# The three-branch merge of a hybrid decoder layer: 24 ordinary tiles with operands split once, in place of twelve seven-product pairs

## The chip, the cores and the metric

The kernel runs on one core of a Trainium2 chip. The metric is the device time of one launch in microseconds. Three runs of the kernel before took 1910.48, 1914.8 and 1914.9 us (median 1914.8). The engines are named as the profile names them: PE is TensorE's matmul and PEld its weight load, DVE is VectorE, ACT is ScalarE, POOL is GpSimd, SP is SyncE, which here only issues DMAs.

## The reference, cut to what matters

One decoder layer is computed for 1024 prompt tokens and 32 sample tokens, 1056 columns in all, with 1024 model channels:

```
h = rmsnorm(x);  proj = h @ w_in        # feeds three mixers and the gates
oa = attention(...)                     # 512 channels
ob = gated short convolution(...)       # 512 channels
oc = gated DeltaNet(...)                # 512 channels
gates = sigmoid(gl)                     # 3 x 1024 channels
merged = gates[0]*(oa @ w_br_a) + gates[1]*(ob @ w_br_b) + gates[2]*(oc @ w_br_c)
x = x + merged @ w_o
x = x + conv_mlp(rmsnorm(x));  y = rmsnorm(x)
```

The line `merged = ...` is the stage that the change touches. Each branch product takes 512 input channels to 1024 output channels. All data is float32.

## The kernel before, in words

Data stands with channels on the 128 partitions and the 1056 columns in a row. A matmul takes a 128x128 piece of weights and streams columns past it. To keep float32 accuracy every operand x is split in two fp32r numbers: hi, a rounded copy written by ACT (`split`, L217), and lo = x - hi, written by DVE or POOL (L218). One product is then three matmuls: hi by hi, hi by lo, lo by hi.

There are two ways to multiply. The ordinary one is `proj` and `products` (L325): an output tile of 128 channels, three groups of 352 columns, for each group 3 matmuls per 128 input channels into one of three PSUM banks named `mm`, and an evacuation that the caller gives. Its weights come by `job`: `w_load` fetches a tile into one of two buffers `wr`, `w_split` splits it on ACT and POOL into one of two buffers `wh` and one of two `wl`; `run_jobs` loads two tiles ahead and splits one ahead, and `look` does the same from inside another stage.

The other is the class `Pairs` (L1429). It takes two output tiles at a time, cuts weights, operand and output in halves, and forms seven block products in place of eight (`PIECES`). For that it needs sums and differences of weight blocks (`produce`, L1386 to L1392), of operand blocks (`build`, L1315, split in L1305 and L1306), and of the products: three of the seven are first copied to SBUF by ACT (L1438) and added to others by DVE (`summed`, L1457). A product here is 264 columns wide.

Before the merge come nine pairs of gate tiles, the last of them named G26; after it come eight ordinary tiles for `w_o` (`wo_job`), then the MLP, whose up-projection is again pairs. The merge before (`merge_pair`) goes through branch b, then c, then a (numbers 1, 2, 0), four pairs each, twelve in all. A pair has 7 pieces x 2 column halves x 6 matmuls. `load_operand` builds the blocks of a branch beforehand; `load_gate` fetches the gates from DRAM. For each output quarter DVE multiplies the product with the gate (L2007); for c and a POOL adds it to the running sum `macc` (L2013); in branch a ACT and DVE split the sum into `mh` and `ml` (L2020, L2021), the operand of `w_o`. `MADD` and `MLO` say which weight sums and which weight splits of the merge are DVE's; the others are POOL's.

The order on each engine is set by a scheduler that works from the order in which the program emits the instructions, with higher priority for evacuations and weight splits; each engine then works through its list in that order. SP issues all these DMAs from one queue in order. Buffers in SBUF are 46 slots, and a DMA into a slot waits until its last reader is done. Small side work (`bg`, the lanes) is woven in by `bg.tick`.

Of the kernel before, what the change touches and what calls it, by code (L numbers as in the profile page):

```python
# [9 lines left out]
ALU = mybir.AluOpType  # L10
# [145 lines left out]
DPAHEAD, DPADD, DPLO, DTICK = 3, (1, 2, 3, 4), (0,), 6  # L156
HGAP, HSTART = (0.0, 1.5), 12
KEPT = 4
MAHEAD, MADD, MLO = 4, (1, 2), (0, 2, 4, 6)
ORDER = """  # L160
d4 hbd q0 d5 d6 dpairs d7 D0 D2 D8 D10 delta
v k q1 q2 q3 attn_in attn g10 g11 g12 g13 g14
# [11 lines left out]
def trunk(tc, A, O, cst_d):  # L174
# [1119 lines left out]
    def pieces(nk):  # L1294
        return {piece: [None] * (nk // 2) for piece in PIECES}

    def build(bs, p, vp, vq, wait, gap=0):

        t, ta = grab([128, T])
        b11, b12, b21, b22 = vp[0][:, :HT], vp[0][:, HT:T], vq[0][:, :HT], vq[0][:, HT:T]  # L1300
        t1, t2 = t[:, :HT], t[:, HT:T]

        def put(piece, src, eng):
            w = grab([128, T], F32R)
            nc.scalar.copy(w[0][:, :HT], src)  # L1305
# [24 lines left out]
        put("t4", t1, nc.vector)  # L1330
        for x in (ta, vp[1], vq[1]):
            x.drop()
# [119 lines left out]
    def summed(ps, x, more):  # L1452

        if x is None:
            return ps
        dst = (mm_ps() if limit[0] < 4 else bg_ps())[:, :HU] if more else ps
        nc.vector.tensor_tensor(dst, ps, x, op=ALU.add)  # L1457
        return dst
# [397 lines left out]
        return whole_pair(lambda which, t: to_dram(g_d[b][m + which], t), AF.Tanh, 0.5)  # L1856

    def last_gates(j):
        if j + gp.ahead == 6:
            merge_start()  # L1860
        if j == 4:
            load_gate(0)

    def last_d(j):
        if j + dpp.ahead >= 6:
# [56 lines left out]

    ops = {}

    def spare():

        return 2 if at["n"] >= mg.first else 5

    def load_operand(b):

        bs = ops[b] = pieces(4)
        if b == order[0][0]:
            vs = [None] * 4
            for t in range(4):
                yield room2(3)
                vs[t] = grab([128, T])
                dma(vs[t][0], br_d[b][t])
            yield bg.arrived()
            both = [build(bs, p, vs[p], vs[p + 2], lambda: room2(4)(), 0.0) for p in range(2)]
            while both:  # L1940
                for g in both:
                    w = next(g, both)
                    if w is both:
                        both = []
                    else:
                        yield w
        else:
            for p in range(2):
                yield lambda: ready[b]() and room2(3 + spare())()
                vs = [grab([128, T]) for _ in range(2)]  # L1950
                for v, t in zip(vs, (p, p + 2)):
                    dma(v[0], br_d[b][t])
                yield bg.arrived()
                yield from build(bs, p, *vs, lambda: room2(2 + spare())(), 4.5)
        bump(f"op{b}")

    ready = {0: lambda: done.get("att", 0) == 2 * NB + 1, 2: lambda: done.get("oc", 0) == 4}

    mh, ml, macc = [None] * 8, [None] * 8, [None] * 8
    gate = {}  # L1960
    order = [(b, m) for b in (1, 2, 0) for m in range(0, 8, 2)]
    wbr = (A["w_br_a"][0], A["w_br_b"][0], A["w_br_c"][0])
    mg = Pairs(4, [wbr[b][:, m * 128:m * 128 + 256].rearrange("(k p) c -> p k c", p=128) for b, m in order], MAHEAD, 4, MADD, MLO, 6)

    def load_gate(i):
        if i < len(order):
            b, m = order[i]
            for x in (m, m + 1):
                bg.until(room2(1))
                gate[b, x] = grab([128, T])  # L1970
                dma(gate[b, x][0], g_d[b][x])

    def merge_start():
        bg.until(room2(2))
        ms = mg.scratch = [grab([128, SLOT]) for _ in range(2)]
        mg.es = [x[0][:, 0:3 * HU].rearrange("p (a b) -> p a b", b=HU) for x in ms]
        mg.s = [x[0][:, 3 * HU:3 * HU + 256].rearrange("p (a b) -> p a b", b=128) for x in ms]
        mg.load(0)
        mg.produce(0)
        mg.produce(1)  # L1980

    def merge_pair(i):
        b, m = order[i]

        def fn():
            if i == 0:
                for j in range(2, MAHEAD):
                    mg.produce(j)
                sb.drop(16)
                mg.load(1)  # L1990
                sf = ff["states"] = grab([128, 836])
                ff["sf"] = sf[0][:, 0:704].rearrange("p (c r) -> p c r", r=16)
                ff["cw"] = sf[0][:, 704:836]
                bg.add(ffn_in())
            if i % 4 == 0 and i < 8:
                bg.add(load_operand(order[i + 4][0]))
            tt, gt = nc.vector.tensor_tensor, nc.gpsimd.tensor_tensor
            if b == 1:
                for x in (m, m + 1):
                    bg.until(room2(1))  # L2000
                    macc[x] = grab([128, T])

            def out(which, c0, ps, x, more):
                ps = summed(ps, x, more)
                cc = slice(c0, c0 + HU)
                g, acc = gate[b, m + which][0], macc[m + which][0]
                nc.vector.scalar_tensor_tensor((acc if b == 1 else g)[:, cc], g[:, cc], 1.0, ps, op0=ALU.add, op1=ALU.mult)  # L2007
                if b == 1:
                    return
                if c0 % HT == 0:  # L2010
                    return
                cc = slice(c0 - HU, c0 + HU)
                gt(acc[:, cc], acc[:, cc], g[:, cc], op=ALU.add)  # L2013
                if b == 0:
                    if c0 > HT:
                        for y in (mh, ml):
                            bg.until(room2(1))
                            y[m + which] = grab([128, T], F32R)
                    h, l = mh[m + which][0], ml[m + which][0]
                    nc.scalar.mul(h[:, cc], acc[:, cc], 0.5)  # L2020
                    nc.vector.scalar_tensor_tensor(l[:, cc], acc[:, cc], 0.5, f32(h[:, cc]), op0=ALU.mult, op1=ALU.subtract)  # L2021

            def before(piece):
                bg.until(lambda: b in ops and ops[b][piece][1] is not None)

            def after(j, piece):
                if j == 3:
                    load_gate(i + 1)
                if i % 4 == 3:
                    for x in ops[b][piece]:  # L2030
                        x[2].drop()
                if i + 1 == len(order) and j + mg.ahead >= 6:
                    look()

            bg.until(lambda: b in ops)
            mg.run(i, ops[b], out, after, before)
            for x in (m, m + 1):
                gate.pop((b, x))[1].drop()
                if b == 0:
                    macc[x][1].drop()  # L2040
            if i + 1 == len(order):
                for x in mg.scratch:
                    x[1].drop()
        return fn

    mg.first = len(jobs)
    for i in range(len(order)):
        jobs.append((None, -1, lambda wh, wl, fn=merge_pair(i): fn()))

    x1, vs = [None] * 8, {}  # L2050
    ff = {}
# [419 lines left out]
```

## Time and profile before

| | |
|---|---|
| profiled execution | 1915.73 us |
| its span, first to last instruction | 1914.0 us |
| PE busy | 1782.4 us (93%) |
| DVE, ACT, POOL busy | 64%, 43%, 58% |
| last gate pair ends, merge begins | about 938 us |
| last of the merge | about 1104 us |
| `w_o` tiles end | 1188.7 us |

The page's 40 slices are 47.9 us each; the merge fills slices 20 to 22 (counted from 0, 957 to 1101 us) and the end of slice 19. A group row of the trace gives line, engine, operation, output and inputs by name, shapes and count, then busy time, mean time of one, and the idle time before it with what ended it. "Idle before" is only of interest on the engine that sets the end.

### The profile page before, as it was taken

How to read it: one execution, taken by the hardware profiler on the slowest of the kernel's cores; microseconds unless marked ns; L12 is line 12 of the kernel's file. 1: busy time of each engine (PE TensorE's matmuls, PEld its weight loads, DVE VectorE, ACT ScalarE, POOL GpSimd, SP SyncE). 2: the span in 40 equal slices, each digit the busy share in tenths (PEclk: the TensorE clock that was granted, in tenths of full speed). 3: DMA queues.
4: the chain of work that ended last, by engine and by line, in shares of the span. 5: the costliest groups of instructions: out<-in, count | busy, mean ns of one | idle time of the engine just before them, and what ended most of it. 6: DMA issues, size and time to landing. Idle time of an engine off the chain costs nothing.

```text
span 1914.0 us, 34344 instructions
## 1 busy us (share of the span) xinstructions
PE 1782.4 (93%) x13006; PEld 1735.1 (91%) x13006; DVE 1234.3 (64%) x2122; ACT 824.1 (43%) x1780; POOL 1113.7 (58%) x1041
## 2 busy tenths in 40 slices
PE   5889989898999997999988899999999999989997
PEld 4789989798999996999987899999999999989997
DVE  5578812364478779421899956778777778764334
ACT  5445522321244434344653445544554454454433
POOL 3245633334333239886668745988887989434542
PEclk9999999896999997999999999999999999999999
DMA  6312597656556533643462343445454343595513
GB/s 222 98 46 79 186 295 214 176 143 145 152 161 169 150 101 123 238 170 114 164 241 84 108 138 132 129 152 179 142 173 148 126 142 133 224 360 195 180 51 108
DMA packets 293302, 300.84 MB, mean 157 GB/s; under 512 B 56516, under 2 KB 224944, under 8 KB 293120
## 3 DMA queue, kind: packets, MB, share of 16 engines
q1 hardware_dynamic: 233648, 261.94, 42.4%
q10 hardware_dynamic: 59488, 36.70, 6.7%
q8 instruction: 102, 1.67, 0.4%
q14 instruction: 64, 0.52, 0.1%
HBM read 205.30 MB, written 95.28 MB: 157 GB/s over the span
## 4 chain that ended last, share of the span: by engine, by line
PE 44%; DVE 8%; issue 3%; POOL 2%; ACT 2%; DMA 2%; SPq 0%; ACTq 0%; DVEq 0%; POOLq 0%
PE mm L1429 17%; PE bgps L1429 13%; PE mm L325 5%; PE bgps L2347 2%; PE bgps L2349 2%; PE bgps L2348 2%; PE mm L2348 1%; PE mm L2347 1%; PE mm L2349 1%; DVE slot L2007 1%; DVE bgps L1457 1%; DVE slot L1315 1%; DVE wh L218 1%; DVE wl L218 1%; DVE slot L1306 1%
## 5 line engine op out<-in xcount | busy, mean ns | idle before, releaser
L325 PE MATMUL mm<-slot,wh 128*128 128x352 f32 x1920 | 487.6, 333 | 22.1 <-ACT slot L1203 11.8
L325 PEld LDWEIGHTS mm<-slot,wh 128*128 128x128 f32 x1920 | 343.2, 193 | 30.0 <-ACT slot L1203 12.7
L325 PE MATMUL mm<-slot,wl 128*128 128x352 f32 x960 | 317.4, 331 | 1.9 <-POOL wl L218 1.9
L1429 PE MATMUL mm<-slot,wh 128*128 128x264 f32 x1536 | 219.6, 294 | 31.0 <-ACT slot L1438 10.8
L1429 PEld LDWEIGHTS mm<-slot,wh 128*128 128x128 f32 x1536 | 204.7, 197 | 37.0 <-ACT slot L1438 12.7
L1429 PE MATMUL mm<-slot,wl 128*128 128x264 f32 x1464 | 200.7, 287 | 7.7 <-DVE wl L218 4.2
L218 POOL TENSOR_TENSOR wl<-slot,wl 128x512 fp32r<-128x512 f32 (+1 forms) x116 | 154.7, 1334 | 83.0 <-ACT wl L217 62.9
L1429 PEld LDWEIGHTS mm<-slot,wl 128*128 128x128 f32 x1464 | 187.6, 190 | 10.4 <-DVE wl L218 5.0
L218 POOL TENSOR_TENSOR wh<-slot,wh 128x512 fp32r<-128x512 f32 (+1 forms) x103 | 134.1, 1302 | 96.1 <-ACT wh L217 83.9
L325 PEld LDWEIGHTS mm<-slot,wl 128*128 128x128 f32 x960 | 185.2, 193 | 4.1 <-POOL wl L218 2.4
L217 ACT CAST slot<-slot 128x528 fp32r<-128x528 f32 (+4 forms) x212 | 130.5, 636 | 127.0 <-DVE slot L1824 27.9
L218 POOL TENSOR_TENSOR wl<-wr,wh 128x1024 fp32r<-128x1024 f32 x38 | 95.4, 2511 | 152.2 <-ACT wh L217 152.1
L218 DVE TENSOR_TENSOR slot<-slot 128x528 fp32r<-128x528 f32 (+3 forms) x117 | 121.4, 1052 | 88.9 <-ACT slot L217 81.1
L218 POOL TENSOR_TENSOR slot<-slot 128x512 fp32r<-128x512 f32 (+3 forms) x95 | 133.4, 1410 | 77.6 <-ACT slot L217 77.5
L1429 PE MATMUL bgps<-slot,wl 128*128 128x264 f32 x1128 | 153.5, 287 | 2.6 <-DVE slot L2007 2.0
L1429 PEld LDWEIGHTS bgps<-slot,wl 128*128 128x128 f32 x1128 | 145.2, 191 | 3.8 <-DVE slot L2007 2.2
L1429 PE MATMUL bgps<-slot,wh 128*128 128x264 f32 x1080 | 145.1, 285 | 1.4 <-DVE slot L2007 1.2
L1429 PEld LDWEIGHTS bgps<-slot,wh 128*128 128x128 f32 x1080 | 136.9, 189 | 2.2 <-DVE slot L2007 1.7
L2187 DVE SCALAR_TENSOR_TENSOR bgps<-slot,bgps 128x358 f32<-128x358 f32 x240 | 127.3, 591 | 12.9 <-ACT bgps L2185 12.2
L1429 PE MATMUL mm<-slot 128*128 128x264 f32 x936 | 124.8, 284 | 1.2 <-DVE bgps L1457 0.5
L1429 PEld LDWEIGHTS mm<-slot 128*128 128x128 f32 x936 | 118.2, 188 | 1.9 <-DVE bgps L1457 0.7
L217 ACT CAST wh<-slot 128x512 fp32r<-128x512 f32 (+1 forms) x115 | 66.0, 576 | 116.1 <-POOL slot L1390 38.9
(404 smaller groups left out, 3952.4 us busy)
## 6 DMA issues: line engine op xcount, KB each, us to landing
wr<-in_w_in SPq DMA_DIRECT2D x32, 512.0 KB
g_d<-slot SPq DMA_DIRECT2D x24, 528.0 KB
slot<-g_d SPq DMA_DIRECT2D x24, 528.0 KB
ht_d<-slot SPq DMA_DIRECT2D x44, 264.0 KB
slot<-ht_d SPq DMA_DIRECT2D x44, 264.0 KB
wr<-in_ffn_up ACTq DMA_DIRECT2D x22, 512.0 KB
slot<-in_ffn_down SPq DMA_DIRECT2D x22, 512.0 KB
slot<-in_ffn_up ACTq DMA_DIRECT2D x22, 512.0 KB
```

The lines of the kernel that those rows point to most:

```text
L217: nc.scalar.copy(hi, src)
L218: eng.tensor_tensor(lo, src, f32(hi), op=ALU.subtract)
L325: mm(ps[:, :TG], a[:, k, :], b[k][:, cc], start=n == 0, stop=n == last)
L1306: eng.tensor_tensor(w[0][:, HT:T], src, f32(w[0][:, :HT]), op=ALU.subtract)
L1315: sub = lambda out, x, y: nc.vector.tensor_tensor(out, x, y, op=ALU.subtract)
L1429: mm(ps, w[:, x + k, :], b[y][:, c0:c0 + HU], start=not n and piece not in NESTED, stop=n == last, skip_group_check=piece in NESTED)
L1457: nc.vector.tensor_tensor(dst, ps, x, op=ALU.add)
L2007: nc.vector.scalar_tensor_tensor((acc if b == 1 else g)[:, cc], g[:, cc], 1.0, ps, op0=ALU.add, op1=ALU.mult)
L2187: nc.vector.scalar_tensor_tensor(ps, cb[:, a + i:b + i], w(i), ps, op0=ALU.mult, op1=ALU.add)
L2347: mm(ps, hi, bh, start=start, stop=False, skip_group_check=True)
L2348: mm(ps, hi, bl, start=False, stop=False, skip_group_check=True)
L2349: mm(ps, lo, bh, start=False, stop=stop, skip_group_check=True)
```

## The change

The merge becomes 24 jobs of the ordinary kind, one for each branch and output tile, in the same order of branches. `load_operand` now fetches a branch's four operand tiles and splits each once, whole (1056 columns), the lo part on DVE for tiles 0 and 2 and on POOL for 1 and 3. The weight sums, operand sums and sums of products go. Evacuations are 352 columns wide; the running sum is added by POOL in branch c as before and by DVE in branch a. Gates are loaded one tile at a time, two tiles ahead. `last_gates` calls `look` so that the first merge weights are split during G26.

```
-    def load_operand(b):   # blocks for the seven products, by build()
+        for t in range(4):
+            yield lambda: (b == order[0][0] or ready[b]()) and room2(5)()
+            v, hi, lo = sb.take([128, T]), sb.take([128, T], F32R), sb.take([128, T], F32R)
+            dma(v, br_d[b][t])
+            yield bg.arrived()
+            split(v, hi, lo, nc.gpsimd if t % 2 else nc.vector)
+            sb.drop()
+            bs[t] = hi, lo
...
-    order = [(b, m) for b in (1, 2, 0) for m in range(0, 8, 2)]
+    order = [(b, m) for b in (1, 2, 0) for m in range(8)]
-    mg = Pairs(4, [wbr[b][:, m * 128:m * 128 + 256]...], MAHEAD, 4, MADD, MLO, 6)
...
+    def merge_job(i):
+        def fn(wh, wl):
+            if i % 8 == 0 and i < 16:
+                bg.add(load_operand(order[i + 8][0]))
+            load_gate(i + 2)
+            def evac(tg, ps):
+                cc = group(tg)[0]
+                nc.vector.scalar_tensor_tensor((acc if b == 1 else g)[:, cc], g[:, cc], 1.0, ps[:, :TG],
+                                               op0=ALU.add, op1=ALU.mult)
+                if b == 1:
+                    return
+                (nc.gpsimd if b else nc.vector).tensor_tensor(acc[:, cc], acc[:, cc], g[:, cc], op=ALU.add)
+                if b == 0:
+                    nc.scalar.mul(h, acc[:, cc], 0.5)
+                    nc.vector.scalar_tensor_tensor(l, acc[:, cc], 0.5, f32(h), op0=ALU.mult, op1=ALU.subtract)
+            proj(wh, wl, [x[0] for x in ops[b]], [x[1] for x in ops[b]], 4, evac)
...
-    for i in range(len(order)):
-        jobs.append((None, -1, lambda wh, wl, fn=merge_pair(i): fn()))
+    for i, (b, m) in enumerate(order):
+        job(wbr[b][:, m * 128:m * 128 + 128].rearrange("(k p) c -> p k c", p=128), 4, merge_job(i))
```

DVE's list in the midst of the merge, in branch b, in the kernel before. L2007 multiplies with the gate, L1457 adds products, L1306 and L1315 build operand blocks, L218, L1386 and L1388 are weight splits and weight sums. This stretch lies in a pair of branch b:

```order
L218 TENSOR_TENSOR wl<-wr,wl 128x256
L2007 SCALAR_TENSOR_TENSOR slot<-slot,bgps 128x264
L1315 TENSOR_TENSOR slot<-slot 128x528
L1457 TENSOR_TENSOR bgps<-bgps,slot 128x264 x2
L218 TENSOR_TENSOR wh<-slot,wh 128x256
L2007 SCALAR_TENSOR_TENSOR slot<-slot,bgps 128x264 x2
L1306 TENSOR_TENSOR slot<-slot 128x528
L1457 TENSOR_TENSOR bgps<-mm,slot 128x264
L1386 TENSOR_TENSOR slot<-wr 128x256
L1457 TENSOR_TENSOR bgps<-mm,slot 128x264
L2007 SCALAR_TENSOR_TENSOR slot<-slot,bgps 128x264
L218 TENSOR_TENSOR wl<-slot,wl 128x256
```

Between two multiplications with the gate stand sums and splits of three other kinds. The same engine in branches b and c of the changed kernel, where L1972 is the multiplication with the gate and L217 the lo part of an operand tile, and then the beginning of branch a (L1976 adds to the running sum, L1984 is the lo part of the sum):

```order
L1972 SCALAR_TENSOR_TENSOR slot<-slot,mm 128x352 x4
L217 TENSOR_TENSOR slot<-slot 128x1056
L1972 SCALAR_TENSOR_TENSOR slot<-slot,mm 128x352 x6
L217 TENSOR_TENSOR slot<-slot 128x1056
L1972 SCALAR_TENSOR_TENSOR slot<-slot,mm 128x352 x15
L217 TENSOR_TENSOR slot<-slot 128x1056
L1972 SCALAR_TENSOR_TENSOR slot<-slot,mm 128x352 x4
L217 TENSOR_TENSOR slot<-slot 128x1056
L1972 SCALAR_TENSOR_TENSOR slot<-slot,mm 128x352 x20
L1976 TENSOR_TENSOR slot<-slot 128x352
L1984 SCALAR_TENSOR_TENSOR slot<-slot 128x352
L1972 SCALAR_TENSOR_TENSOR slot<-slot,mm 128x352
```

Five kinds of work that stood between two evacuations have left DVE's list; what is left beside them is a handful of operand splits and, in branch a, two more instructions per evacuation.

POOL's list from the first merge weights to the fifth tile of branch c in the changed kernel; wl<-wr,wh is the lo part of one merge tile's weights, 128x1056 that of an operand tile, L1976 the running sum:

```order
L217 TENSOR_TENSOR wl<-wr,wh 128x512 x4
L217 TENSOR_TENSOR slot<-slot 128x1056
L217 TENSOR_TENSOR wl<-wr,wh 128x512 x2
L217 TENSOR_TENSOR slot<-slot 128x1056
L217 TENSOR_TENSOR wl<-wr,wh 128x512 x4
L1976 TENSOR_TENSOR slot<-slot 128x352 x3
L217 TENSOR_TENSOR slot<-slot 128x1056
L217 TENSOR_TENSOR wl<-wr,wh 128x512
L1976 TENSOR_TENSOR slot<-slot 128x352 x2
L217 TENSOR_TENSOR wl<-wr,wh 128x512
L1976 TENSOR_TENSOR slot<-slot 128x352 x2
L217 TENSOR_TENSOR slot<-slot 128x1056
```

The weights of the third tile of branch c (the eleventh split) now stand behind three additions of the first tile and behind an operand split.

## Rows read from the trace of the kernel before

**Rows 1.** The page: engine totals, and the chain that ended last by engine.

```profile
PE 1782.4 (93%) x13006; PEld 1735.1 (91%) x13006; DVE 1234.3 (64%) x2122; ACT 824.1 (43%) x1780; POOL 1113.7 (58%) x1041
...
PE 44%; DVE 8%; issue 3%; POOL 2%; ACT 2%; DMA 2%; SPq 0%; ACTq 0%; DVEq 0%; POOLq 0%
```

**Rows 2.** Stretches: length; busy (count) PE, PEld, DVE, ACT, POOL; clock, DMA share, GB/s.

```profile
938.00:1104.00 166.00, 144.95 (x1064) 138.09 (x1063) 160.03 (x286) 79.38 (x207) 121.31 (x104) 0.96 0.41 144
1104.00:1180.00 76.00, 76.00 (x477) 75.74 (x476) 46.06 (x64) 35.38 (x57) 31.60 (x17) 1.00 0.43 142
```

**Rows 3.** What PE waited for from 938 to 1104 us: total, times, longest.

```profile
PE mm L1429 <- DVE bgps L1457: 6.3, 5, 2.6
PE mm L1429 <- DVE wl L218: 4.2, 4, 1.8
PE bgps L1429 <- DVE slot L2007: 3.2, 3, 2.0
PE mm L1429 <- DVE wh L218: 2.6, 3, 1.5
PE mm L1429 <- ACT slot L1438: 2.1, 3, 0.9
PE mm L325 <- DVE slot L2007: 1.2, 1, 1.2
PE mm L1429 <- DVE slot L2007: 1.1, 4, 0.4
```

**Rows 4.** The pairs' matmuls (L1429) alone: stretch, length, busy (count) PE, PEld.

```profile
0.00:938.00 938.00, 278.86 (x2185) 275.72 (x2186) 0.95 0.53 157
860.00:920.00 60.00, 60.00 (x494) 59.86 (x493) 1.00 0.31 106
```

**Rows 5.** The ordinary matmuls (L325) alone by stretch.

```profile
938.00:1104.00 166.00, 8.26 (x47) 7.53 (x48) 0.96 0.41 144
1104.00:1180.00 76.00, 76.00 (x477) 75.74 (x476) 1.00 0.43 142
```

**Rows 6.** The transposes (L383) alone from 938 to 1104 us.

```profile
938.00:1104.00 166.00, 1.88 (x8) 1.07 (x8) 0.96 0.41 144
```

**Rows 7.** DVE's groups from 938 to 1104 us, each shape apart.

```profile
L2007 DVE SCALAR_TENSOR_TENSOR slot<-slot,bgps 128x264 f32<-128x264 f32 x72 | 29.4, 419 | 0.3
L1457 DVE TENSOR_TENSOR bgps<-bgps,slot 128x264 f32<-128x264 f32 x48 | 20.0, 430 | 3.2 <-PE bgps L1429 1.8 <-ACT slot L1438 1.4
L1315 DVE TENSOR_TENSOR slot<-slot 128x528 f32<-128x528 f32 x16 | 17.0, 1084 | 0.0
```

**Rows 8.** From the views of lines L1315, L218 and L686: ns min/median/max.

```profile
L1315 DVE TENSOR_TENSOR slot<-slot x40: 693/1174/1840, 909.9 to 1194.2; 128x528 f32<-128x528 f32 x40
...
L218 POOL TENSOR_TENSOR wl<-slot,wl x116: 732/1291/2369, 126.1 to 1846.6; 128x512 fp32r<-128x512 f32 x104, 128x256 fp32r<-128x256 f32 x12
...
L686 POOL TENSOR_TENSOR slot<-slot x4: 2475/2484/3333, 225.9 to 242.7; 128x1056 f32<-128x1056 f32 x4
```

**Rows 9.** Groups from 700 to 900 us (DVE) and 700 to 1104 us (ACT).

```profile
L218 DVE TENSOR_TENSOR slot<-slot 128x1056 fp32r<-128x1056 f32 x4 | 9.1, 2306 | 1.5 <-ACT slot L217 1.3
L1465 DVE SCALAR_TENSOR_TENSOR slot<-slot,mm 128x352 f32<-128x352 f32 x3 | 1.4, 508 | 0.0
...
L217 ACT CAST wh<-slot 128x512 fp32r<-128x512 f32 x14 | 8.7, 620 | 14.7 <-PE bgps L1429 4.2 <-POOL slot L1390 3.3 <-POOL slot L1392 3.0
```

**Rows 10.** POOL's running sum from 938 to 1104 us.

```profile
L2013 POOL TENSOR_TENSOR slot<-slot 128x528 f32<-128x528 f32 x32 | 47.2, 1488 | 13.1 <-DVE slot L2007 13.1
```

**Rows 11.** PE in order of time at 1041 and 1050 us: start, us, matmuls.

```profile
1041.97 1.63 PE L1429 MATMUL mm<-slot,wl 128*128 128x264 f32 x12
...
1049.23 0.75 PE L1429 MATMUL mm<-slot,wl 128*128 128x264 f32 x4 [1.76 <-DVE wl L218]
...
1050.85 2.85 PE L1429 MATMUL mm<-slot,wl 128*128 128x264 f32 x12
```

**Rows 12.** The chain in order of time, 935 to 1110 us: a weight load.

```profile
954.51 4.07 DMA wr<-in_w_br_b
```

More of the change, by code (lines that the diff above doesn't have):

```diff
@@ L158 @@
 KEPT = 4
-MAHEAD, MADD, MLO = 4, (1, 2), (0, 2, 4, 6)
 ORDER = """
@@ L1858, in last_gates @@
     def last_gates(j):
[L1859 to L1862, printed above, removed]
+        if j + gp.ahead >= 6:
+            look()
+        if j in (4, 5):
+            load_gate(j - 4)
     def last_d(j):
@@ L1923, in trunk @@
     ops = {}
-    def spare():
-        return 2 if at["n"] >= mg.first else 5
     def load_operand(b):
[L1931 to L1937, printed above, removed]
-            yield bg.arrived()
[L1939 to L1954, printed above, removed]
+        bs = ops[b] = [None] * 4
+        for t in range(4):
+            yield lambda: (b == order[0][0] or ready[b]()) and room2(5)()
+            v, hi, lo = sb.take([128, T]), sb.take([128, T], F32R), sb.take([128, T], F32R)
+            dma(v, br_d[b][t])
+            yield bg.arrived()
+            split(v, hi, lo, nc.gpsimd if t % 2 else nc.vector)
+            sb.drop()
+            bs[t] = hi, lo
+            yield
         bump(f"op{b}")
@@ L1960, in trunk @@
     gate = {}
-    order = [(b, m) for b in (1, 2, 0) for m in range(0, 8, 2)]
+    order = [(b, m) for b in (1, 2, 0) for m in range(8)]
     wbr = (A["w_br_a"][0], A["w_br_b"][0], A["w_br_c"][0])
-    mg = Pairs(4, [wbr[b][:, m * 128:m * 128 + 256].rearrange("(k p) c -> p k c", p=128) for b, m in order], MAHEAD, 4, MADD, MLO, 6)
     def load_gate(i):
         if i < len(order):
[L1967 to L1982, printed above, removed]
+            bg.until(room2(1))
+            gate[order[i]] = sb.take([128, T])
+            dma(gate[order[i]], g_d[order[i][0]][order[i][1]])
+    def merge_job(i):
         b, m = order[i]
-        def fn():
+        def fn(wh, wl):
             if i == 0:
-                for j in range(2, MAHEAD):
-                    mg.produce(j)
                 sb.drop(16)
-                mg.load(1)
                 sf = ff["states"] = grab([128, 836])
@@ L1994, in fn @@
                 bg.add(ffn_in())
-            if i % 4 == 0 and i < 8:
-                bg.add(load_operand(order[i + 4][0]))
-            tt, gt = nc.vector.tensor_tensor, nc.gpsimd.tensor_tensor
+            if i % 8 == 0 and i < 16:
+                bg.add(load_operand(order[i + 8][0]))
             if b == 1:
[L1999 to L2007, printed above, removed]
+                bg.until(room2(1))
+                macc[m] = grab([128, T])
@@ L2008, in out @@
+            bg.until(lambda: done.get(f"op{b}"))
+            load_gate(i + 2)
+            g, acc = gate.pop((b, m)), macc[m][0]
+            def evac(tg, ps):
+                cc = group(tg)[0]
+                nc.vector.scalar_tensor_tensor((acc if b == 1 else g)[:, cc], g[:, cc], 1.0, ps[:, :TG],
+                                               op0=ALU.add, op1=ALU.mult)
                 if b == 1:
                     return
-                if c0 % HT == 0:
-                    return
-                cc = slice(c0 - HU, c0 + HU)
@@ L2013, in out @@
-                gt(acc[:, cc], acc[:, cc], g[:, cc], op=ALU.add)
+                (nc.gpsimd if b else nc.vector).tensor_tensor(acc[:, cc], acc[:, cc], g[:, cc], op=ALU.add)
                 if b == 0:
-                    if c0 > HT:
+                    if tg == 0:
                         for y in (mh, ml):
                             bg.until(room2(1))
[L2018 to L2043, printed above, removed]
-        return fn
-    mg.first = len(jobs)
-    for i in range(len(order)):
-        jobs.append((None, -1, lambda wh, wl, fn=merge_pair(i): fn()))
+                            y[m] = grab([128, T], F32R)
+                    h, l = mh[m][0][:, cc], ml[m][0][:, cc]
@@ new lines, in evac @@
+                    nc.scalar.mul(h, acc[:, cc], 0.5)
+                    nc.vector.scalar_tensor_tensor(l, acc[:, cc], 0.5, f32(h), op0=ALU.mult, op1=ALU.subtract)
+            proj(wh, wl, [x[0] for x in ops[b]], [x[1] for x in ops[b]], 4, evac)
+            sb.drop()
+            if b == 0:
+                macc[m][1].drop()
+            if i % 8 == 7:
+                sb.drop(8)
+        return fn
+    for i, (b, m) in enumerate(order):
+        job(wbr[b][:, m * 128:m * 128 + 128].rearrange("(k p) c -> p k c", p=128), 4, merge_job(i))
```

## The prediction

> **What bounds the kernel now.** I read the page first. PE is busy 93% of the span and holds 44% of the chain that ended last [rows 1], so a change pays only as far as it shortens what PE does or waits for. Then I cut the span where the change acts. The last gate pair ends at 938 us: up to there 2185 of the pairs' matmuls have run, and 13 pairs of 168 are 2184 [rows 4]. By 1104 us the merge is over. The reader is to see in the table of stretches that in these 166.0 us DVE is busy 160.03 us, 96%, while PE is busy 144.95; in the `w_o` tiles right behind, PE is busy all of 76.00 us and DVE 61% [rows 2]. So this one stretch is bound by DVE, in a kernel bound by PE elsewhere. The waits of PE in it agree: 20.7 us, of which 18.6 end with a DVE instruction (6.3 sums of products, 6.8 weight splits, 5.5 multiplications with the gate) and 2.1 with an ACT copy [rows 3].
>
> **What the stretch costs on PE.** Undisturbed, a pair's matmul takes 60.00/494 = 0.1215 us [rows 4] and an ordinary one 76.00/477 = 0.1593 us [rows 5]; the busy column can't be used, since neighbours overlap. The merge before has 12 x 7 x 2 x 6 = 1008 matmuls: 122.4 us. Beside them stand 47 ordinary matmuls of the first `w_o` tile, 7.5 us [rows 5], and 8 transposes, 1.9 us [rows 6]. That is 131.8, so 34.2 of the 166.0 us are lost. 21.0 of them are PE's idle time (166.0 less 144.95); up to 6.6 are clock: it was granted at 0.96 in the mean [rows 2], and behind a wait of 1.76 us twelve matmuls take 2.85 us that take 1.63 elsewhere, 1.2 in place of 2.4 GHz [rows 11]. The rest is slow restarts.
>
> **The change on PE.** Added: 24 tiles x 3 column groups x 12 = 864 matmuls at 0.1593, 137.6 us. Removed: the 1008, 122.4 us. PE's own work grows by 15.2 us. If nothing is lost any more the stretch takes 137.6 + 7.5 + 1.9 = 147.0 us in place of 166.0: 19.0 us less. So all hangs on how much of the 34.2 us stays.
>
> **The change on the other engines.** DVE loses 72 sums of products (430 ns), 96 evacuations at 264 columns (419 ns), its weight sums and weight splits, and the operand blocks (1084 ns for 528 columns) [rows 7]. It gains 72 evacuations of 352 columns, whose form stands in the trace at 508 ns [rows 9]: 36.6 us. In branch a it gains 48 operations on SBUF alone. 528 columns of these take 693 ns at best [rows 8], and a column about 1.01 ns (508 less 419 over 88), so I estimate 0.515 us each, 24.7 us. Six operand splits at up to 2.31 us [rows 9], of which the order shows four inside the stretch, are 9.2. Together 70.5 of 147 us, 48% in place of 96%. Nothing of DVE's 18.6 us must stay.
>
> POOL gets 24 weight splits at 1.29 us [rows 8], 24 additions at 352/528 x 1488 = 0.99 us [rows 10], and operand splits at 2.48 to 3.33 [rows 8], four of them inside: about 65 us, where it was busy 121 [rows 2]. ACT loses 72 copies and 84 small weight casts for 24 casts of 0.62 [rows 9] and 12 operand casts; it was half idle before. DMA moves the same bytes: 24 loads of 256 KB for twelve of 512 KB, the same gates and operands. 144 GB/s over 166 us are 163 over 147, the share 0.41 becomes about 0.46 [rows 2]. These edits I cost at nothing; PE's stream hides them, and the next part says where that cover is thin.
>
> **Where the new stretch can lose.** First the handover of weights. The split of tile i+1 starts when tile i-1 gives its buffers back, that is at the start of tile i, and takes ACT 0.62 and POOL 1.29 us, 1.9 of the 5.73 us (36 x 0.1593) that tile i lasts. There are 3.8 us to spare, as long as neither engine's list puts something long ahead. One place does: the eleventh split, for the third tile of branch c, stands behind the first tile's third addition and an operand split (POOL's order). From the end of that first tile it is evacuation 0.51, addition 0.99, operand split 2.48 to 3.33, weights 1.29, 5.3 to 6.1 us against 5.73: 0 to 0.4 us late; I take 0.5 with semaphores. Behind this split wait later additions, for which nobody hurries. Second, the start: the first tile's weights are split in G26's last pieces, the second's only when G26 has ended, 1.9 us into 5.73. ACT's casts of operands stand between casts of weights and wait for DMAs; a late one would hold the weights behind it. I take 1 us. Third, branch a on DVE: 0.51 + 2 x 0.515 = 1.54 us per group of 1.91 us, 4.6 per tile.
>
> Operations with one input in PSUM keep their time whatever POOL does (419 ns on average for 264 columns [rows 7], in a stretch where POOL is busy 73%); those on SBUF alone spread from 693 to 1840 ns [rows 8]. The Trainium skill, "SBUF — State Buffer", section "Who interferes with whom", calls the port pair of VectorE and GpSimd an exclusive lock, held for a whole instruction against an operation with two SBUF inputs; the spread agrees with it. By that rule a weight split of POOL can stop DVE for 1.29 us per tile of branch a. A stop of that length would make DVE's tile 5.9 us, 0.2 over PE's, 1.4 us in eight tiles; with no stop it is 0. I take 1 us, nearer the stop, since the spread exceeds 1 us.
>
> Sum of the losses: 0.5 + 1 + 1 = 2.5 us. Bounds: 0 below (what is left is then PE streaming at a rate measured with DVE and POOL at work, so I see no further gain), and above 12.3 us, if PE's waits for weight splits (6.8) and for evacuations (5.5) stay as large as they are [rows 3]; the waits for sums of products and copies have no successor. I take a value near 0 because the `w_o` tiles, with the same helper, the same banks, the same two buffers and weights at the same rate (512 KB in two such tile times), lose nothing [rows 5].
>
> **Sum.** -19.0 + 2.5 = -16.5 us: 1915.73 becomes 1899.2 for the profiled execution. That one lies 0.9 us over the median of the runs shown, so I say 1898.5 for the median. Behind the stretch `w_o` is unchanged; the order of the other engines differs only here and in a few neighbours of the last phase, and the wait at the start of the up-projection moves forward as it is. What is late next is PE itself.
>
> **Rivals.** *Waits of the kept kinds stay.* Evacuations and weight splits lose 12.3 us as now; 1915.7 - 19.0 + 12.3 - 0.9 = 1908. For it: two buffers only, and tiles half as long as those of `w_o`. Against it: all those waits ended on an engine 96% busy.
>
> *The clock stays down.* If short waits at each of the 72 bank changes kept the granted clock at 0.90, the 137.6 us would be 152.9, 15.3 more: 1898.5 + 15.3 = 1914, no change. Against it: `w_o` changes the same three banks under a clock of 1.00 [rows 2]; its groups are twice as long, though. The Trainium skill, "TensorE: Matmul & The Clock Gate", section "A second HAM failure mode: psum-queue depth-cycling", tells of a kernel whose clock swung because it cycled banks; by that rule this rival holds, and the `w_o` rows disagree with it.
>
> *Weights come late, and the kernel is slower.* The place is SP's one queue. A buffer `wr` turns once in two tiles, 11.46 us: POOL frees it, a load of up to 4.07 us (for 512 KB) [rows 12], the cast, the split, 6.0 us in all. SP works in order, and gates and operands wait there for slots in between. Each load that comes x us late beyond the 5.5 spare us costs PE x/2 per tile. From 19.0/24 = 0.8 us per tile on the gain is gone, and at 1.5 us per tile it is 36 - 19.0 - 0.9 = 16 slower, 1932. Against it: a load is asked for more than a tile ahead, and queue and bytes are those of now.
>
> **Chances.** Forecast, losses of 0 to 8 us (1896 to 1904): 0.71. Kept waits (1904 to 1909): 0.13. Clock or anything else that eats the gain: 0.08. Late weights, or another mishap that makes it slower: 0.08. I count 0.3%, 5.7 us, as what a measurement of this kernel can tell from no change; below 1909.1 is faster: 0.84; same 0.08; slower 0.08. The range reaches up to the kept waits, 1909, and down to 1892, since one run shown was 1910.5 and 19.0 less is 1891.5.
>
> **What would show it.** Right: from the last pair of gates to the first matmul of `w_o`'s second tile about 149 us in place of 166; 864 ordinary matmuls more, at 0.16 us each; DVE about half busy there; granted clock 1.00; PE's waits there under 5 us. Wrong steps: waits of PE on POOL's or ACT's weights every tile (late weights), on L1972 in branch a (DVE), a granted clock under 0.95, or a rate other than 0.1593. The prediction fails if DVE's share falls to half and the stretch still takes 160 us or more.

## The result and the profile after

The changed kernel takes 1890.7 us (median; 1889.6 to 1894.2), the kernel before 1914.85 in the runs beside it: ratio 0.988, 95% interval 0.986 to 0.990. It is 24 us faster where I had said 16, and 1.3 us below my range. The profiled span is 1888.0 us in place of 1914.0.

The page's engine totals and the chain by engine, after (they answer to [rows 1]):

```profile
PE 1781.3 (94%) x12862; PEld 1741.7 (92%) x12862; DVE 1127.3 (60%) x1944; ACT 778.3 (41%) x1626; POOL 1061.4 (56%) x985
...
PE 50%; DVE 3%; DMA 2%; ACT 2%; POOL 2%; issue 1%; SPq 0%; DVEq 0%; ACTq 0%; POOLq 0%
```

PE is busy for as long as before, but its idle time falls from 131.6 to 106.7 us of the span. DVE's part of the chain falls from 8% to 3%, PE's rises from 44% to 50%.

The merge after, from its first matmul on, and the `w_o` tiles behind it (columns as in [rows 2]):

```profile
933.50:1080.00 146.50, 146.50 (x920) 145.88 (x919) 70.45 (x125) 38.09 (x67) 69.76 (x53) 1.00 0.50 168
1080.00:1164.60 84.60, 84.60 (x532) 84.60 (x531) 49.10 (x68) 38.96 (x62) 38.57 (x21) 1.00 0.38 128
```

PE is busy for all of 146.50 us, at a granted clock of 1.00. The view of PE's waits, which filled [rows 3] before, has no row between 933.4 and 1165 us. DVE is busy 48% of the stretch in place of 96%.

DVE's groups of the merge after, each shape apart, then POOL's (they answer to [rows 7, 8, 10]):

```profile
L1972 DVE SCALAR_TENSOR_TENSOR slot<-slot,mm 128x352 f32<-128x352 f32 x72 | 37.4, 520 | 72.7 <-PE mm L324 72.6
L1976 DVE TENSOR_TENSOR slot<-slot 128x352 f32<-128x352 f32 x24 | 15.8, 660 | 0.2
L1984 DVE SCALAR_TENSOR_TENSOR slot<-slot 128x352 fp32r<-128x352 f32 x24 | 15.6, 649 | 2.3 <-ACT slot L1983 1.3
L217 DVE TENSOR_TENSOR slot<-slot 128x1056 fp32r<-128x1056 f32 x4 | 5.1, 1273 | 1.1 <-ACT slot L216 1.1
```

```profile
L217 POOL TENSOR_TENSOR wl<-wr,wh 128x512 fp32r<-128x512 f32 x23 | 31.3, 1360 | 65.1 <-ACT wh L216 59.9 <-DVE slot L1972 5.2
L1976 POOL TENSOR_TENSOR slot<-slot 128x352 f32<-128x352 f32 x24 | 24.4, 1034 | 4.1 <-DVE slot L1972 4.1
L217 POOL TENSOR_TENSOR slot<-slot 128x1056 fp32r<-128x1056 f32 x4 | 9.9, 2471 | 0.3 <-ACT slot L216 0.3
```

DVE's evacuations (L1972) now wait for PE: 72.6 us of its idle time end with PE. That is the sign that the bound has changed sides: before, PE waited for DVE [rows 3]. The evacuation comes at 520 ns (508 in [rows 9]); the operations on SBUF alone at 650 and 660 ns, over my 515, and the operand splits at 1273, under the 2306.

### The profile page after: what moved, and what is told of

Its sections match the earlier page's. It is cut to its first block, busy times and chain, and to the rows that moved or that the text cites. A ratio compares the mean times of both kernels' runs of the same rounds, so it can differ in the third digit from the quotient of the medians.

```text
span 1888.0 us, 33612 instructions
## 1 busy us (share of the span) xinstructions
PE 1781.3 (94%) x12862; PEld 1741.7 (92%) x12862; DVE 1127.3 (60%) x1944; ACT 778.3 (41%) x1626; POOL 1061.4 (56%) x985
## 4 chain that ended last, share of the span: by engine, by line
PE 50%; DVE 3%; DMA 2%; ACT 2%; POOL 2%; issue 1%; SPq 0%; DVEq 0%; ACTq 0%; POOLq 0%
PE mm L1428 16%; PE mm L324 12%; PE bgps L1428 12%; PE bgps L2294 2%; PE bgps L2296 2%; PE bgps L2295 2%; PE mm L2295 1%; PE mm L2296 1%; PE mm L2294 1%; DVE slot L2134 1%; DMA slot<-hb_d 1%; DMA wr<-in_ffn_up 1%; DVE slot L2176 1%; DMA st_d<-slot 0%; ACT slot L216 0%
## 5 line engine op out<-in xcount | busy, mean ns | idle before, releaser
L324 PE MATMUL mm<-slot,wh 128*128 128x352 f32 x2496 | 625.3, 331 | 19.6 <-ACT slot L1202 10.9
L324 PEld LDWEIGHTS mm<-slot,wh 128*128 128x128 f32 x2496 | 442.8, 192 | 27.0 <-ACT slot L1202 11.7
L324 PE MATMUL mm<-slot,wl 128*128 128x352 f32 x1248 | 409.7, 328 | 1.9 <-POOL wl L217 1.9
L217 POOL TENSOR_TENSOR wl<-wr,wh 128x1024 fp32r<-128x1024 f32 (+1 forms) x62 | 127.1, 2050 | 233.3 <-ACT wh L216 224.1
L217 POOL TENSOR_TENSOR slot<-slot 128x512 fp32r<-128x512 f32 (+4 forms) x101 | 148.6, 1478 | 84.6 <-ACT slot L216 77.9
L1428 PE MATMUL mm<-slot,wh 128*128 128x264 f32 x1248 | 172.7, 291 | 17.7 <-ACT slot L1437 8.6
L217 DVE TENSOR_TENSOR slot<-slot 128x528 fp32r<-128x528 f32 (+3 forms) x123 | 130.3, 1073 | 94.2 <-ACT slot L216 87.5
L217 POOL TENSOR_TENSOR wl<-slot,wl 128x512 fp32r<-128x512 f32 x104 | 145.8, 1402 | 71.6 <-ACT wl L216 63.7
L1428 PEld LDWEIGHTS mm<-slot,wh 128*128 128x128 f32 x1248 | 163.0, 194 | 20.8 <-ACT slot L1437 9.9
L217 POOL TENSOR_TENSOR wh<-slot,wh 128x512 fp32r<-128x512 f32 x91 | 122.3, 1343 | 90.6 <-ACT wh L216 74.5
L1428 PE MATMUL mm<-slot,wl 128*128 128x264 f32 x1176 | 155.3, 284 | 0.6 <-ACT slot L1437 0.6
L216 ACT CAST wh<-wr 128x512 fp32r<-128x512 f32 (+1 forms) x94 | 75.2, 800 | 161.6 <-PE mm L324 124.1
L2134 DVE SCALAR_TENSOR_TENSOR bgps<-slot,bgps 128x358 f32<-128x358 f32 x240 | 127.3, 588 | 11.8 <-ACT bgps L2132 11.0
```

Of the source, the lines that this page charges most:

```text
L324: mm(ps[:, :TG], a[:, k, :], b[k][:, cc], start=n == 0, stop=n == last)
L1428: mm(ps, w[:, x + k, :], b[y][:, c0:c0 + HU], start=not n and piece not in NESTED, stop=n == last, skip_group_check=piece in NESTED)
L2134: nc.vector.scalar_tensor_tensor(ps, cb[:, a + i:b + i], w(i), ps, op0=ALU.mult, op1=ALU.add)
```

## The experiments

Each profile is cut at the same events: the end of the last gate pair's matmuls, and the last matmul of `w_o`. Between them lies the **stage**: the merge and `w_o`. It is 251.0 us before and 231.4 after, 19.6 less.

**e0 and e1: both kernels again, unchanged.**

> The kernel before, unchanged, against itself: it shows how far executions of one program lie apart, and where. If the 6 us by which the change gained more than its stage shows (4.4 us before the merge begins, 1.9 us behind w_o) are spread between executions, this run begins the merge anywhere between 933 and 938 us, and its ratio is 1.000 within 0.2%. If they belong to the change, it begins the merge at 938 us again and has about 725 us from the end of w_o to the end of the span.

> The changed kernel again, in more rounds. If the gain is the stage's alone: 19 to 21 us, ratio 0.989 to 0.990, with the merge beginning anywhere between 933 and 938 us. If something outside the stage gains too: 24 us, ratio 0.9875, the merge begins at 933.5 us again, and 723 us follow w_o.

Measured: 1912.84 us against 1913.19 for the kernel before (ratio 1.0002 [0.9989, 1.0015]), and 1890.05 (0.989 [0.987, 0.991]). The stages are 250.9 and 231.7: they repeat to 0.3 us, so a stage tells a difference of one us where the whole time does not. What lies around the stage doesn't repeat so well, in instructions that both programs issue in nearly the same order on PE: over the two kernels and experiments the merge began between 933.4 and 940.7 us, and the time from the end of `w_o` to the end was 720.8 to 725.7 us in either. The 4.4 us by which the merge began earlier in the first profile after are thus no proof of a gain; in the second pair it is 2.4.

**e2: 24 of 48 weight splits of the merge from DVE to POOL**

```
-MAHEAD, MADD, MLO = 4, (1, 2), (0, 2, 4, 6)
+MAHEAD, MADD, MLO = 4, (1, 2), (0, 2)
```

> The kernel before, seven-product pairs kept, with 24 of the merge's 48 weight splits moved from DVE to POOL (two of its four pieces). DVE has about 20 us less in the stretch (160 to 140), POOL about 23 more (121 to 144). If DVE's total is what held PE up: the stretch of 166 us falls to 148 to 152, 14 to 18 us faster, with DVE and POOL both over 90% busy. If single late handovers hold PE up, whoever does them: within 4 us of before. If POOL's longer weight splits only take over as the thing waited for: slower by up to 8 us.

Measured: ratio 0.9981 [0.9966, 0.9996], stage 247.1, 3.9 us less. That is what single late handovers were to give (within 4 us), not the 14 to 18 us of a stretch held up by DVE's total. DVE lost only some 10 us, not 20: from 938.6 to 1100 us it is still 93% busy, with POOL at 86%.

**e3: no sums of products**

```
-                ps = summed(ps, x, more)
```

> The kernel before with the merge's 72 sums of products left out (DVE multiplies each product with the gate as it is, so the merge's output is not the reference's); PE's matmuls, weight work and operand blocks stay. DVE has 30 us less in the stretch. If DVE's total bounds it: 166 us falls to 134 to 140 (131.8 is PE alone), 26 to 30 us faster, faster than the changed kernel too. If the chain of pieces (product, copy, sum, bank free) or the weights bound it: 5 to 12 us faster, and PE waits for weight splits instead.

Measured: ratio 0.9958 [0.9943, 0.9973], stage 245.0, 6.0 less. 72 instructions of 0.43 us are gone from the engine that I had called the bound, and four fifths of that time came to nothing. "DVE's total bounds the stage" had fallen in this form, and the further runs take other work away.

**e6 and e7: operand blocks built once, weights prepared once**

```
-        bs = ops[b] = pieces(4)
+        bs = ops[b] = pieces(4) if b == order[0][0] else ops[order[0][0]]
...
+            if h == 2 and q:               # e7, in produce()
+                self.items[j] = self.w0[i]
```

> The kernel before, with the operand blocks of branches c and a left out: all three branches multiply with branch b's blocks, so their loads, casts, sums and splits go (the products of c and a are other numbers). DVE loses 2 x 16 instructions of 1.08 us, 35 us, in the merge, more than with the sums of products (31 us, 6.0 us shorter); POOL loses 12 splits of some 2.5 us, 30; ACT 28 casts. Theory 1, whatever takes time from DVE gives back about the same share, 0.2 to 0.3 us per us as in the two experiments before: 7 to 10 us shorter. Theory 2, it is these long instructions (1.1 us on DVE, 2.5 to 3.3 on POOL, several pieces of PE's 1.46 us each) behind which the weights and evacuations wait: 12 to 19 us shorter, and PE's waits on weight splits gone. Theory 3, it is the 84 hand-overs of weights themselves: under 5 us.

> The kernel before, with the merge's weights prepared once: the seven items of the first pair serve all twelve pairs, so that 77 casts, 44 weight sums and 77 splits go (44 splits and 22 sums from DVE, some 35 us; 33 splits and 22 sums from POOL, some 45; the loads stay, and the other pairs multiply with the first one's weights). Theory 1, share of DVE's time, 0.2 to 0.3 us per us: 7 to 10 us shorter. Theory 3, the hand-overs of weights are what PE waits for (6.8 of 20.7 us end with a weight split, with the clock behind them): 12 to 19 us shorter. Theory 2, the long instructions of the operand blocks: under 5 us, as then evacuations are late in place of weights.

Measured: e6 ratio 0.989 [0.987, 0.992], stage 230.9, 20.1 less; e7 0.987 [0.984, 0.989], stage 228.2, 22.8 less. Either alone gives more than the 12 to 19 us that theories 2 and 3 gave to one of them only; both theories fall as "the one cause". The parts overlap: losses of 34.2 us can't hold 20 and 23 side by side.

**e8, e9, e10, e11: which engine's part.** From the kernel before are left out POOL's part of the blocks (e8), DVE's part of them (e9), POOL's additions (e10), and these with the sums of products (e11).

```
+            if gap and eng is nc.gpsimd:       # e8; e9: nc.vector, and no sub()
+                lo = w[0][:, :HT]
...
-                gt(acc[:, cc], acc[:, cc], g[:, cc], op=ALU.add)      # e10, e11
-                ps = summed(ps, x, more)                              # e11
```

> The kernel before, without POOL's part of the operand blocks of branches c and a: 12 splits of 528 columns, 18.4 us of POOL at 1.53 us; matmuls read the high part in place of the low one (other numbers, as many matmuls). Without all of the blocks' work (35 us of DVE, 18 of POOL, 17 of ACT) the stretch from the last gate pair to the end of w_o was 20.0 us shorter, without the sums of products (31 us of DVE) only 6.0. Theory A, POOL and DVE hinder each other, so that POOL's time on long SBUF operations counts as DVE's: 4 to 8 us shorter, and DVE's operations on SBUF alone shorter on average. Theory B, DVE's list alone: 0 to 2. Theory C, the blocks' instructions stand in the way at their places in the lists, on whichever engine: half of the 20, 8 to 12.

> The kernel before, without DVE's part of the operand blocks of branches c and a: 16 subtractions and 16 splits of 528 columns, 32 us of DVE at 1.08 and 0.95 us; the blocks are then the raw quarters, the low parts of four of the seven are their high parts (other numbers, as many matmuls); POOL's splits and ACT's casts stay. As much of DVE as with the sums of products, which gave 6.0. Theory A (POOL and DVE hinder each other): 8 to 12 us shorter, since these operations wait for POOL where the sums, with an input in PSUM, don't. Theory B, DVE's total counts whatever the operation: 6. Theory C (the blocks' places in the lists): 12 to 18, nearly all of the 20.

> The kernel before, without POOL's 32 additions to the accumulators in branches c and a (1.49 us each, 47.6 us of POOL; the sum over the branches is then branch b's alone). DVE, ACT and PE keep every instruction. Theory A, POOL's SBUF operations stretch DVE's (0.69 us at best, 1.08 to 1.28 on average): DVE's busy time in the stretch falls from 161 to some 145, and the stretch is 10 to 16 us shorter. Theory B, DVE's list alone: 0 to 3. Theory C, the blocks' places: 0 to 4.

> The kernel before without the 72 sums of products on DVE and without POOL's 32 additions (both left out of the computation): 31 us off DVE and 47 off POOL, and none of the weights' or blocks' work. Theory A: more than the two apart, 16 to 22 us shorter than before, as much as with the blocks left out. Theory B: about 6 to 9. Theory C, the blocks stand in the way: 6 to 10, with PE's waits on weight splits left.

| left out | off DVE, us | off POOL, us | stage, us | less than 251.0 | ratio [95%] |
|---|---|---|---|---|---|
| e3: sums of products | 31 | 0 | 245.0 | 6.0 | 0.996 [0.994, 0.997] |
| e8: POOL's block splits | 0 | 18 | 246.7 | 4.3 | 0.997 [0.996, 0.998] |
| e9: DVE's block work | 32 | 0 | 232.2 | 18.8 | 0.991 [0.989, 0.993] |
| e10: POOL's additions | 0 | 48 | 234.5 | 16.5 | 0.992 [0.990, 0.994] |
| e11: sums and additions | 31 | 48 | 226.9 | 24.1 | 0.987 [0.985, 0.989] |

e10 is the clearest. DVE keeps all its instructions, and yet the stage falls by 16.5 us. DVE's lo parts of the merged result before (L2021):

```profile
L2021 DVE SCALAR_TENSOR_TENSOR slot<-slot 128x528 fp32r<-128x528 f32 x16 | 20.5, 1280 | 2.0 <-ACT slot L2020 1.9
```

The same 16 instructions in e10 (L2020 there), and its sums on PSUM:

```profile
L1457 DVE TENSOR_TENSOR bgps<-bgps,slot 128x264 f32<-128x264 f32 x48 | 20.2, 429 | 5.6 <-ACT slot L1438 3.1 <-PE bgps L1429 2.3
...
L2020 DVE SCALAR_TENSOR_TENSOR slot<-slot 128x528 fp32r<-128x528 f32 x16 | 11.8, 756 | 0.0
```

Most operations on SBUF alone become shorter when POOL does less: beside these lo parts the weight splits (1006 to 706 ns and 901 to 685 for the two forms of `wl`). The block operations do not (1084 to 1041, 945 to 1080); POOL's own block splits still run beside them. Those with an input in PSUM stay at 430 and 429 ns. All engines from 938.5 to 1110 us, before and in e10 (columns as in [rows 2]):

```profile
938.50:1110.00 171.50, 150.45 (x1096) 143.33 (x1095) 161.62 (x289) 81.42 (x211) 122.68 (x105) 0.96 0.41 146
```

```profile
938.50:1110.00 171.50, 159.68 (x1197) 153.93 (x1196) 144.74 (x298) 88.15 (x218) 81.95 (x76) 1.00 0.46 162
```

DVE's busy time falls from 161.6 to 144.7 us, as theory A had it (145), though the window holds nine more of its instructions in e10, where the kernel is further on. DVE stood idle for only 6 us of the 166 before [rows 2], so waits between its instructions can't have given the 16.5 us.

The trace of the kernel before shows the same by itself. The merge has 48 DVE operations of 128x528 on SBUF alone (L1306, L1315, L2021). Nine ran beside no POOL instruction and took 694 to 707 ns; the 39 others took 695 to 2576, 1196 on average. Of the 70 of 128x256 (L218, L1386, L1388) 18 ran beside none and took 409 to 426 ns; the other 52 took 411 to 1573, 963 on average. Two of the lo parts on DVE, and what POOL did beside the second (it did nothing beside the first):

```profile
1072.15 0.70 DVE L2021 SCALAR_TENSOR_TENSOR slot<-slot 128x528 fp32r<-128x528 f32 x1
...
1091.72 2.58 DVE L2021 SCALAR_TENSOR_TENSOR slot<-slot 128x528 fp32r<-128x528 f32 x1
```

```profile
1090.85 2.88 POOL L218 TENSOR_TENSOR wl<-wr,wh 128x1024 fp32r<-128x1024 f32 x1
```

The durations of DVE's instructions from 937.8 to 1104 us sum to 181 us (more than the 160 busy, since neighbours overlap). With the median that each form takes beside no POOL instruction (for some forms one to three cases) they would sum to 133. So by this estimate some 48 us were stretching by POOL inside DVE's instructions, and DVE's own work was about 112 us of the 160, less than PE's own 131.8.

Theory A also gave e8 (4 to 8, measured 4.3); e10 and e11 lie a little over what it gave (10 to 16 and 16 to 22) and far over theories B and C. For e9 its 8 to 12 were too few and theory C's 12 to 18 nearer, though 18.8 is over these too, so where the work stands counts as well.

The place is seen when the merge is cut at every second pair, 168 matmuls, 20.4 us undisturbed. The kernel before (columns as in [rows 2]), in the order b, b, c, c, a, a:

```profile
937.80:959.60 21.80, 21.80 (x179) 21.40 (x178) 20.50 (x43) 14.67 (x45) 13.53 (x15) 1.00 0.52 178
959.60:983.70 24.10, 21.85 (x170) 20.73 (x169) 24.06 (x51) 13.07 (x34) 13.42 (x14) 1.00 0.54 197
983.70:1014.40 30.70, 23.71 (x171) 22.13 (x170) 30.70 (x52) 14.84 (x37) 22.00 (x18) 0.94 0.56 214
1014.40:1041.90 27.50, 23.70 (x171) 22.31 (x170) 26.79 (x47) 10.66 (x29) 23.28 (x21) 0.94 0.24 78
1041.90:1067.40 25.50, 22.93 (x169) 22.09 (x169) 24.09 (x45) 11.43 (x31) 21.51 (x21) 0.93 0.35 128
1067.40:1096.80 29.40, 25.19 (x182) 23.95 (x181) 27.52 (x48) 12.96 (x30) 20.37 (x16) 0.94 0.28 88
```

DVE is 94 to 100% busy in every one, and POOL 69 to 85% from the third on, where the long losses are. Without POOL's additions (e10):

```profile
958.30:982.40 24.10, 21.86 (x171) 20.74 (x170) 24.06 (x50) 13.06 (x34) 13.43 (x14) 1.00 0.54 200
982.40:1009.20 26.80, 22.48 (x171) 20.83 (x169) 26.80 (x49) 15.07 (x37) 15.87 (x15) 1.00 0.63 243
...
1058.20:1079.90 21.70, 21.62 (x177) 21.41 (x176) 16.22 (x40) 8.79 (x22) 6.18 (x7) 1.00 0.24 69
```

The second section, where POOL has no additions in either, is unchanged at 24.10; the third loses 3.9 us and the last 7.7, with DVE down to 75% there. Without the sums (e3):

```profile
961.50:982.00 20.50, 20.50 (x171) 20.50 (x170) 18.14 (x34) 12.46 (x33) 12.67 (x13) 1.00 0.46 160
982.00:1016.10 34.10, 26.94 (x170) 25.21 (x169) 32.58 (x45) 14.96 (x38) 25.95 (x21) 0.83 0.51 195
...
1061.80:1092.00 30.20, 24.63 (x179) 23.26 (x179) 25.55 (x37) 15.57 (x35) 25.37 (x20) 0.97 0.30 98
```

The second section is now free of loss, and the fifth nearly so; but the third grew from 30.7 us (32.1 in e0, the same kernel again) to 34.1, with DVE busy for longer on fewer instructions. DVE in order of time in it, in e3, and POOL beside it (start, duration, count):

```profile
1002.52 2.98 DVE L1315 TENSOR_TENSOR slot<-slot 128x528 f32<-128x528 f32 x2
1005.43 1.83 DVE L1306 TENSOR_TENSOR slot<-slot 128x528 fp32r<-128x528 f32 x1
1007.18 0.42 DVE L2006 SCALAR_TENSOR_TENSOR slot<-slot,bgps 128x264 f32<-128x264 f32 x1
```

```profile
1002.28 1.49 POOL L2012 TENSOR_TENSOR slot<-slot 128x528 f32<-128x528 f32 x1
1003.73 1.21 POOL L218 TENSOR_TENSOR wh<-wr,wh 128x256 fp32r<-128x256 f32 x1
1004.90 1.79 POOL L2012 TENSOR_TENSOR slot<-slot 128x528 f32<-128x528 f32 x1
1006.65 1.78 POOL L1306 TENSOR_TENSOR slot<-slot 128x528 fp32r<-128x528 f32 x1
```

Three block operations of 0.69 us at best [rows 8] take 4.8 us while POOL goes from one instruction to the next; the evacuation at 1007.18 stands behind them. Sums with an input in PSUM are work that DVE can do beside POOL, so taking them away leaves DVE in POOL's way instead. That this explains the growth, 2.0 to 3.4 us, is my reading of one execution.

**e4: two more additions on DVE per evacuation, in the changed kernel**

```
+                for _ in range(2):
+                    nc.vector.tensor_tensor(spin["t"][:, cc], g[:, cc], g[:, cc], op=ALU.add)
```

> The changed kernel, with two more additions of 352 columns on DVE behind each of the merge's 72 evacuations (144 in all, on SBUF alone, into a tile that nothing reads; the results stay the same). Theory 1, DVE's throughput is what bounds a stage of this kind, and PE is late only where DVE's work per column group is longer than PE's: the evacuation takes 0.52 us, an addition 0.52 to 0.66, so a group of branches b and c costs DVE 1.55 to 1.85 of the 1.91 us that PE takes: no waits there. A group of branch a costs 0.52 + 0.66 + 0.65 + 1.03 to 1.3 = 2.9 to 3.1 us, 0.95 to 1.2 over PE's: 24 groups give 23 to 29 us, 1913 to 1919 in all, with all of PE's waits in branch a and on the evacuation. Theory 2, single hand-overs (an instruction that stands at the wrong place in the list, or is stretched by POOL) make the waits and not the total: PE waits in branches b and c as well, 0.5 us or more per tile (8 us or more over the two), and branch a costs under 20.

Measured: 1917.1 us against 1913.6 for the kernel before; the stage is 261.0, 29.6 longer than after. Branches b, c and a:

```profile
940.75:994.16 53.41, 50.08 (x299) 48.39 (x298) 42.06 (x73) 10.73 (x21) 17.74 (x10) 0.97 0.56 187
994.16:1051.91 57.75, 51.18 (x290) 47.05 (x289) 54.77 (x66) 9.02 (x12) 44.26 (x31) 0.97 0.40 136
1051.91:1107.47 55.56, 49.28 (x290) 45.81 (x290) 55.32 (x106) 14.90 (x28) 18.73 (x11) 1.00 0.33 106
```

In the changed kernel they last 47.3, 46.0 and 45.9 us. The profiled execution was the slowest of ten (1924.7 us), so these times may lie over a usual run's; by the medians the additions cost 26 to 27 us. The gain can be undone by work on DVE alone, but not where theory 1 said: branch c loses most, 11.8 us, at a DVE busy 95% with POOL at 77%, and branch b 6.1 at a DVE busy 79%. Branch a loses 9.6, not the 23 to 29 of theory 1. Theory 2 told the places. An average that fits (1.55 to 1.85 of 1.91 us) doesn't suffice if instructions stretch while POOL works.

**e5: branch b as pairs, c and a as ordinary tiles**

```
+    order = [(1, m) for m in range(0, 8, 2)]
+    tiles = [(b, m) for b in (2, 0) for m in range(8)]
```

> Branch b as four pairs of the kernel before, branches c and a as 16 ordinary tiles of the changed one. PE's own work is 4 x (72 x 0.1593 - 84 x 0.1215) = 4 x 1.27 = 5.1 us less than in the changed kernel. If the pairs lose only while blocks for the next branch, gate work and sums coincide (theory: the loss comes from what is beside them, and is small where POOL and DVE have no additions and no blocks of their own kind), branch b loses 0 to 2 us and the kernel is 3 to 5 us faster than the changed one, 1885 to 1888. If every pair loses its share of the 34.2 us, 2.85 each, it is 11.4 - 5.1 = 6 us slower than the changed one, about 1896.

Measured: 1889.6 us, ratio 0.987 [0.985, 0.989]; stage 229.4, 2.0 under the changed kernel. The time can't be told from the changed kernel's. PE has 5.1 us less to do and gets 2.0 of it. Branch b's pairs take 46.4 us where their 336 matmuls and 8 transposes would take 42.7, a loss of some 3.6: more than the 0 to 2 of the one forecast, far less than the 11.4 of the other. Pairs pay a little in the branch where POOL has no additions. None of the versions with the whole computation is shown to beat the changed kernel.

## Why the prediction was wrong, point by point

- **PE's own work, right.** The stage gave 19.6 and 19.2 us, where I had worked out 19.0 for no losses. At my rates the changed stage is 137.6 + 1.9 + 91.8 (the 576 matmuls of `w_o`) = 231.3 us; it measured 231.4 and 231.7. In the changed kernel branch c's 288 matmuls take 46.0 us, 0.1597 each, against my 0.1593.
- **"Where the new stretch can lose", wrong: 2.5 us, measured 0.** This is the term of the sum for the stretch that failed; it is 2.5 of the 7.8 us that I was off, and the last point has the rest. The place on POOL came as the order had shown it. POOL in order of time after, the first tile's third addition in branch c, the operand split and the weights of the third tile:

```profile
987.42 0.95 POOL L1976 TENSOR_TENSOR slot<-slot 128x352 f32<-128x352 f32 x1 [0.98 <-DVE slot L1972]
988.33 2.46 POOL L217 TENSOR_TENSOR slot<-slot 128x1056 fp32r<-128x1056 f32 x1
990.75 1.30 POOL L217 TENSOR_TENSOR wl<-wr,wh 128x512 fp32r<-128x512 f32 x1
```

  From 987.42 to 992.05 it is 4.6 us, and with the evacuation ahead 5.1, under 5.73; I had allowed for an operand split of up to 3.33. The start and branch a, 1 us each, cost nothing either: DVE's 36.4 us in branch a's 45.9 hold some stretching: 43 of its 48 operations on SBUF alone took 0.51 to 0.60 us, five 1.62 to 2.24, all five beside POOL. Such stops came, but none reached PE.
- **DVE and POOL, right in sum and by luck in part.** I had 70.5 and about 65 us, the trace has 70.45 and 69.76 busy (DVE's durations sum to 74, the figure to hold against my sum, since neighbours overlap). On DVE the operations on SBUF alone came out 6.7 us over my 24.7, the operand splits 4.1 under.
- **"This one stretch is bound by DVE", too coarse.** DVE was full, section by section, but part of the 96% was waiting for POOL inside its instructions, some 48 us by the estimate above. e10 shows it: POOL's additions gone, DVE's list the same, 16.5 us. Work taken off DVE alone gave as much (e9, 18.8) or little (e3, 6.0). The change thinned both engines; how its gain divides between them isn't shown.
- **The stretching, known but put in the wrong place.** The lo parts of 128x528 on SBUF alone go from 1280 to 756 ns with POOL's additions gone, while sums with an input in PSUM stay at 430 and 429. The Trainium skill, "SBUF — State Buffer", section "Who interferes with whom", says that VectorE and GpSimd share a port pair that one of them locks; the traces agree in kind. I used the stretching for 1 us of the new stretch, and did not see that it lay behind much of the 34.2 us lost before (16.5 us go with POOL's additions, e10).
- **The rivals.** Kept waits: none of the 12.3 us is left. The clock that stays down: granted 1.00 over all 72 changes of bank. The Trainium skill, "TensorE: Matmul & The Clock Gate", section "A second HAM failure mode: psum-queue depth-cycling", tells of a clock that swung under such cycling through banks; this trace disagrees. Late weights on SP: no wait on weights.
- **The rest, and the range.** With losses of 0 the sum would have said 1895.8, inside my range, so the losses alone don't explain a time below it. Of the 7.8 us that I was off, 2.5 are the losses and some 0.5 the stage. The base was high: the kernel before has medians of 1912.0 to 1913.6 in later comparisons, 1.2 to 2.8 under the 1914.8 from which I started, and runs down to 1905.8 us. That leaves 2 to 4 us in a term that I put at nothing, all that lies outside the stage ("the wait at the start of the up-projection moves forward as it is"). By the medians the changed kernel gains 4.6 and 3.9 us more than its stage in the two comparisons; for the eight variants of the kernel before (e2, e3, e6 to e11) the two differ by -2.8 to +2.5 us. The profiles don't settle it: the time outside the stage is 1656.6 and 1657.5 us for the changed kernel, 1657.3 to 1664.3 in ten profiles of the kernel before and its variants. 19.4 us of 1913.2 is a ratio of 0.990, inside both intervals. So a gain beyond the stage is likely but not shown, and its cause stays open. My low end was the lowest of three runs less the gain, with nothing for medians that move by 2 us between comparisons.

## What to carry to other kernels

When an engine is near 100% busy, ask how much of that is its own work: compare the mean of its SBUF-only instructions with their minimum, and look at which engine was busy beside them. Leave out one engine's work at a time, and cut the stretch at equal counts of PE's work: an average over the stage hides that each section has another bottleneck, and gains of single edits need not add (e6 and e7 give 42.9 us by themselves, where 34.2 were lost; e3 and e10 nearly add, 22.5 against 24.1 in e11). Where a loss-free stretch of the same helper stands in the trace, its rate and its zero loss are the better guess (here they gave 231.3 us against 231.4), and the uncertainty belongs into the base.

## What the runs showed that I had not expected

- Taking 31 us of work off an engine 96% busy shortened the stage by 6.0 us; taking 48 us off the other engine, busy 73%, by 16.5.
- Leaving out the sums of products made one section longer, 30.7 or 32.1 to 34.1 us.
- With the weights prepared once (e7), the first section lasts 25.3 us in place of 21.8, at a DMA share of 0.98 in place of 0.52. PE has one wait in it, 1.9 us on a DMA (`slot<-scw_d`, a load for the MLP), and the granted clock is 0.93. That loads which no longer wait for their buffers run ahead of what is needed first is my reading.
